# A two-layer hybrid backbone: the token mixers' TensorE work put in a fixed order, with split attention scores and stacked S5 halves

## The chip, the cores and the metric

The kernel runs on one core of one Trainium2 chip. The metric is device time in microseconds of one execution, from the core's first to its last instruction and what lies around it. Engines are named as in the profile: PE (TensorE matmul), PEld (its weight loads), DVE (VectorE), ACT (ScalarE), POOL (GpSimd), SP (the queue that issues most transfers).

## The reference

Two layers act on 256 latent tokens and 256 context tokens, 1024 channels wide, batch 1, all in float32. Each layer is a half-step SwiGLU feed-forward block (hidden width 2816), a block of parallel token mixers, and another half-step feed-forward block. Every block's input is normalised and modulated by vectors made from a conditioning vector; its output is scaled by a modulation gate, added to the stream and normalised.

The mixer block projects its modulated input once (`w_in`) into five parts and runs three branches on them:

- **S5**: 16 groups of 16 channels, a bidirectional complex diagonal state space with 64 states each; the scan over the context tokens hands its state to the latent tokens. A tanh-GELU and a gated linear unit (`w_glu`) follow.
- **FNet**: a 2-D DFT over positions and the 64 channels of each of 4 groups, real part.
- **Neighbourhood attention**: 8 heads of 64 channels, axial rotary position code, a window of 8 rows by 16 columns with a learned bias, plus all 256 context keys in the same softmax. In the first layer the context tokens attend among themselves too; the last layer makes no context output, so its queries, FNet and gates cover 256 tokens and not 512.

Each branch is projected to 1024 channels, multiplied by its own sigmoid gate (three gate vectors from `w_in`), the three are summed and projected by `w_out`.

## The kernel before

**Precision.** A large product is made of three matmuls on float32r parts: the weights (`chunk`, L79 and L80) and the activations are split into a high and a low part, and `mm3` (L87 to L89) issues high by high, high by low, low by high. Small products (S5, the DFT, attention scores and values) are plain float32 matmuls; a row of the profile with `x2` or `x8` counts two matmul records for each of those.

**The mixer in stages.** `mixer` opens a *front*: a main stream and side streams. The main stream is `main()`: the projections for S5 and half of the values (`tiled`, PSUM tile `pgm`), FNet (`pgf`), then for each of four head pairs the keys (`pgk`) and queries (`pgq`), the other half of the values, and the gate columns of the first output tiles (`pgg`, `gate_cols`). In the first layer (T = 512) the front prepares gate tiles 0 and 1, in the second (T = 256) tiles 0, 1 and 2. `interleave` advances the main stream by one yield a round (12 matmuls of 512 columns, or 24 of 256), and then each side stream whose count has run down; a yielded number is the rounds until its next turn.

The side streams are `ssm_stream` (S5 in two halves of 128 channels: eight transposes `psu` per half, then for each of four units `ssm_s2`, tile `psv`, and `ssm_s3`, tile `psy`, then GELU in `ssm_half` and eight transposes `psyt`; at the end `glu`, tile `psz`), `fnet` (`psf`, `pso`), one `attention` stream for each head pair, and `more`, which runs the steps of `extra` every third round.

`attention` takes a pair's keys and queries from PSUM, turns them by the rotary code (`rope`), and goes through jobs (head, query tile): `softmax_x` issues one float32 scores matmul (64 rows by 512 columns, tile `pss`) and the softmax on DVE and ACT; `softmax_c` does so for the context queries (two matmuls of 256 columns, `psc`); `transpose_p` turns the probabilities (`ppt`). At each turn it issues the scores of the next job and the transposes of the current one:

```
first(0)
for j in range(len(jobs)):
    yield 1
    if j + 1 < len(jobs):
        first(j + 1)
    second(j)
yield 1
nc.scalar.copy(yN[:, pair, :T], pv()[:, :T])
```

`pv` multiplies by the values (tile `po`): two heads in two column halves of the array, alternating.

`merge` follows: all branch outputs are split into `bh` (L1286, L1287), and for each of eight output tiles `d` it issues the gate columns of `d + 1`, then the three branch products (`pdb`), which DVE multiplies with the gates and adds. Then `w_out` (`pd` from `yT`) with the block's end.

**Modulation.** `mod(l, n)` makes 512 modulation values on DVE: four steps, each a 512 KB load on the SP queue into one of four `raw` buffers that weights share, and four products of 512 elements with a sum (L190). The first layer's mixer is given five such vectors (`M(0, 11, 16)`, 20 steps) as `extra`; the second's none.

**Order.** Nothing in the program fixes the order on any engine, apart from a few marked places: a list scheduler orders each engine's instructions ahead of time by program order as priority, by its own estimate of when operands are ready, and by free buffers. The order in the program is only a preference there. PSUM in the front: three buffers `psg`, three `psa` (scores, transposes, `po`), two `pss` (S5, and scratch of `mod`).

Of the kernel before, what the change touches and what calls it, by code (L numbers as in the profile page):

```python
# [8 lines left out]
F32 = mybir.dt.float32  # L9
F32R = mybir.dt.float32r  # L10
# [8 lines left out]
KT = 8  # L19
# [4 lines left out]
S_C, S_T, S_R, SN = 512, 1088, 1600, 1604  # L24


class Kernel:
    def __init__(self, tc, ctx, I, out):
# [8 lines left out]
        self.held = {}  # L37
        self.ctxs = ctx.enter_context(ExitStack())
# [137 lines left out]
    def mod(self, l, n):  # L176
# [7 lines left out]
        for b in range(4):  # L184
            raw = self.wraw.tile([128, 1024], F32, name="raw", tag="raw")
            nc.sync.dma_start(raw, I["w_modT"][l, n, b])
            junk = self.side([128, 512], "pj")
# [633 lines left out]
    def ssm_s2(self, l, pool, u, U):  # L821
# [13 lines left out]
        H = T("H", [128, 4, 64], 2)  # L835
# [3 lines left out]
        for c in range(4):  # L839
            g = 2 * (u % 4) + c % 2  # L840
            rhs = U[:, g].rearrange("p (h n) -> p h n", h=2)[:, ::-1, :] if c < 2 else U[:, g, ::-1]
# [16 lines left out]
        return st, mt, H, U  # L858

    def ssm_s3(self, u, q, yh, NR):  # L860

        nc = self.nc
        st, mt, H, U = q
        ca = st[:, S_C:S_C + 576].rearrange("p (c j k) -> p c j k", c=4, j=9)
        py = self.pss.tile([128, 128], F32, name="psy", tag="s")
        for i in range(3):
            for g in range(2):
                lhs, rhs = ((U[:, 2 * (u % 4) + g], mt[:, g]), (H[:, g], ca[:, g, 1:9]),
                            (H[:, 2 + g], ca[:, 2 + g, 0:8]))[i]
                nc.tensor.matmul(py[64 * g:64 * g + NR], lhs[:, :NR], rhs, start=i == 0, stop=i == 2,  # L870
                                 tile_position=(0, 64 * g))
        for g in range(2):
            ch = 32 * (u % 4) + 16 * g
            nc.scalar.copy(yh[:NR, :, ch:ch + 16], py[64 * g:64 * g + NR].rearrange("n (t c) -> n t c", t=8))

    def ssm_stream(self, l, pool, zt, yS, T):

# [3 lines left out]
        yh = {}  # L881
# [3 lines left out]
        yield 6 if l == 0 else 4  # L885

        def load(hf):
            zr = pool.tile([64, 8, 128], F32, name="zr", tag="ga", bufs=1)
            nc.sync.dma_start(zr, zv[:, :, 128 * hf:128 * hf + 128])
            Zs = pool.tile([64, 8, 8, 16], F32, name="Zs", tag="Zs", bufs=1)  # L890
            nc.scalar.copy(Zs, zr.rearrange("n s (g c) -> n g s c", g=8)[:, :, ::-1])
            yh[hf] = pool.tile([64, 8, 128], F32, name="yh", tag="yh", bufs=1)
            yield 1
            pu = self.pss.tile([128, 8, 64], F32, name="psu", tag="s")
            for g in range(8):
                nc.tensor.transpose(pu[:, g], Zs[:, g].rearrange("n s c -> n (s c)"), self.ident[:64, :64])
            U = pool.tile([128, 8, 64], F32, name="U", tag="U", bufs=1)
            nc.scalar.copy(U, pu)
            yield 1
            return U  # L900

        q = {}
        for hf in range(2):
            U = yield from load(hf)
            for u in range(4 * hf, 4 * hf + 4):
                q[u] = self.ssm_s2(l, pool, u, U)
                yield 1
                if u % 4:
                    self.ssm_s3(u - 1, q.pop(u - 1), yh[hf], NR)
                    yield 1  # L910
            self.ssm_s3(u, q.pop(u), yh[hf], NR)
            yield from self.ssm_half(l, pool, yh[hf], yS[:, hf, :T], NR)
        yield 1
        self.glu(l, pool, yS, T)

# [591 lines left out]
```

## Time and profile before

| | us |
|---|---|
| median of three runs (2030.26 to 2035.7) | 2033.48 |
| the profiled execution | 2028.64 |
| its span, first to last instruction | 2026.9 |
| first layer's front, 412.7 to 626.2 | 213.5 |
| first layer's merge, 626.2 to 768.3 | 142.1 |
| second layer's front, 1570.4 to 1733.0 | 162.6 |
| second layer's merge, 1733.0 to 1805.0 | 72.0 |

Starts are counted from the span's first instruction. A matmul's record is longer than the time until the next one starts, since matmuls are pipelined; so the cost of a matmul in a stream is read as the distance between two starts, and a busy PE can still be going slowly.

### The profile page before, as it was taken

The numbers are of one execution on the slowest core, as the hardware profiler recorded it, in microseconds if no ns is written. First come the engines' busy times: TensorE is split into PE (matmuls) and PEld (weight loads), VectorE is DVE, ScalarE is ACT, GpSimd is POOL, SyncE is SP. The second block draws the span as 40 slices with busy tenths as digits, with TensorE's granted clock in tenths as the row PEclk, the third lists the DMA queues.
The fourth block names the chain that finished last, engine by engine and source line by source line (L and its number), as shares of the span: only waits on it lengthen the run. The fifth ranks groups of instructions, "written<-read, shape, count | busy, mean of one in ns | idle before, by whom it ended". The sixth has DMA issues, their size and how long they took to land.

```text
span 2026.9 us, 27725 instructions
## 1 busy us (share of the span) xinstructions
PE 1970.7 (97%) x10072; PEld 1613.4 (80%) x10072; DVE 1526.9 (75%) x3405; ACT 777.1 (38%) x1253; POOL 111.6 (6%) x185
## 2 busy tenths in 40 slices
PE   7999999999999999999999999999999999999997
PEld 4888887787767887888888878888887977987886
DVE  4996899868997337876899688669768787775555
ACT  4322232355654224422233243222224566544442
POOL 0000100011000000100000010000001110000000
PEclk9999999999999999999999999999999999999999
DMA  8445556455344323345465625446543643664563
GB/s 317 151 148 156 174 200 206 151 175 171 118 145 140 104 88 123 124 152 181 154 209 184 221 94 187 156 155 206 171 159 117 200 150 124 206 218 149 185 179 122
DMA packets 103113, 333.03 MB, mean 164 GB/s; under 512 B 12352, under 2 KB 25504, under 8 KB 102976
## 3 DMA queue, kind: packets, MB, share of 16 engines
q1 hardware_dynamic: 96384, 310.96, 47.1%
q10 hardware_dynamic: 3584, 14.24, 1.9%
q0 software_dynamic: 3008, 6.07, 1.0%
q8 instruction: 79, 1.29, 0.3%
q14 instruction: 58, 0.48, 0.1%
HBM read 313.70 MB, written 17.51 MB: 163 GB/s over the span
## 4 chain that ended last, share of the span: by engine, by line
PE 59%; DVE 7%; issue 3%; DMA 2%; ACT 2%; POOL 1%; SPq 0%; POOLq 0%; ACTq 0%; DVEq 0%
PE pg L87 4%; PE pu L87 4%; PE pg L88 4%; PE pu L88 4%; PE pu L89 4%; PE pg L89 4%; PE pd L89 4%; PE pd L88 4%; PE pd L87 4%; PE pgg L87 3%; PE pgg L89 3%; PE pgg L88 3%; PE pgu L87 2%; PE pgu L88 2%; PE pgu L89 2%
## 5 line engine op out<-in xcount | busy, mean ns | idle before, releaser
L79 ACT CAST whi<-raw 128x1024 fp32r<-128x1024 f32 (+1 forms) x380 | 390.7, 1032 | 615.6 <-PE pd L89 154.9
L80 DVE TENSOR_TENSOR wlo<-raw,whi 128x1024 fp32r<-128x1024 f32 (+1 forms) x380 | 454.1, 1198 | 213.5 <-ACT whi L79 210.1
L190 DVE SCALAR_TENSOR_TENSOR pj<-raw,cb 128x512 f32<-128x512 f32 x512 | 350.5, 704 | 48.7 <-DMA raw<-in_w_modT 45.1
L87 PE MATMUL pd<-whi,gT 128*128 128x512 f32 x616 | 240.8, 391 | 0.4 <-DVE ev L273 0.4
L88 PE MATMUL pd<-wlo,gT 128*128 128x512 f32 x616 | 240.6, 391 | 0.5 <-DVE wlo L80 0.5
L89 PE MATMUL pd<-whi,gT 128*128 128x512 f32 x616 | 239.4, 389 | 0.0
L87 PE MATMUL pg<-uhi,whi 128*128 128x512 f32 (+1 forms) x560 | 215.1, 384 | 4.6 <-ACT uhi L247 4.4
L89 PE MATMUL pg<-uhi,wlo 128*128 128x512 f32 (+1 forms) x560 | 211.8, 378 | 2.7 <-DVE wlo L80 2.7
L87 PE MATMUL pu<-uhi,whi 128*128 128x512 f32 (+1 forms) x560 | 212.3, 379 | 1.3 <-DVE q L294 1.3
L88 PE MATMUL pg<-ulo,whi 128*128 128x512 f32 (+1 forms) x560 | 212.3, 379 | 0.0
L88 PE MATMUL pu<-ulo,whi 128*128 128x512 f32 (+1 forms) x560 | 211.8, 378 | 0.0
L89 PE MATMUL pu<-uhi,wlo 128*128 128x512 f32 (+1 forms) x560 | 211.7, 378 | 0.0
L87 PEld LDWEIGHTS pd<-whi,gT 128*128 128x128 f32 x616 | 115.6, 188 | 26.3 <-DVE ev L273 0.8
L88 PEld LDWEIGHTS pd<-wlo,gT 128*128 128x128 f32 x616 | 115.7, 188 | 24.6 <-DVE wlo L80 1.2
L89 PEld LDWEIGHTS pd<-whi,gT 128*128 128x128 f32 x616 | 115.7, 188 | 23.9
L87 PE MATMUL pgg<-uhi,whi 128*128 128x512 f32 (+1 forms) x384 | 131.8, 343 | 0.0
L89 PE MATMUL pgg<-uhi,wlo 128*128 128x512 f32 (+1 forms) x384 | 130.2, 340 | 0.5 <-DVE wlo L80 0.4
L88 PE MATMUL pgg<-ulo,whi 128*128 128x512 f32 (+1 forms) x384 | 129.7, 338 | 0.0
L87 PEld LDWEIGHTS pg<-uhi,whi 128*128 128x128 f32 x560 | 106.2, 190 | 28.9 <-ACT uhi L247 4.9
L89 PEld LDWEIGHTS pg<-uhi,wlo 128*128 128x128 f32 x560 | 105.9, 189 | 22.4 <-DVE wlo L80 3.1
L87 PEld LDWEIGHTS pu<-uhi,whi 128*128 128x128 f32 x560 | 106.2, 190 | 21.3 <-DVE q L294 1.5
L88 PEld LDWEIGHTS pg<-ulo,whi 128*128 128x128 f32 x560 | 105.9, 189 | 20.5 <-issue 1.2
(600 smaller groups left out, 3469.5 us busy)
## 6 DMA issues: line engine op xcount, KB each, us to landing
raw<-in_w_gu SPq DMA_DIRECT2D x132, 512.0 KB
raw<-in_w_modT SPq DMA_DIRECT2D x128, 512.0 KB
raw<-in_w_dn SPq DMA_DIRECT2D x80, 512.0 KB
raw<-in_w_in SPq DMA_DIRECT2D x80, 512.0 KB
raw<-in_w_gul SPq DMA_DIRECT2D x44, 512.0 KB
sd<-sst ACTq DMA_DIRECT2D x16, 802.0 KB
sst<-sd SPq DMA_DIRECT2D x16, 802.0 KB
wm<-in_w_mod SPq DMA_DIRECT2D x16, 512.0 KB
```

Of the source, the lines that this page charges most:

```text
L79: nc.scalar.copy(hi[:, :m], raw[:, :m])
L80: nc.vector.tensor_sub(lo[:, :m], raw[:, :m], hi[:, :m].bitcast(F32))
L87: mm(ps, a[0], b[0], start=start, stop=False)
L88: mm(ps, a[0], b[1], start=False, stop=False)
L89: self.last = mm(ps, a[1], b[0], start=False, stop=stop)
L190: V.scalar_tensor_tensor(junk, raw[:, 512 * k:512 * k + 512], 1.0, self.cb[:, s, 512 * k:512 * k + 512], op0=OP.mult, op1=OP.mult, accum_o ...
```

## The change

It touches the two mixers only:

1. From the second round of `main` on, the front runs under `manual_schedule` for PE, and so does `merge`: PE takes its instructions in program order. The other engines are scheduled as before.
2. Attention becomes one stream over all pairs. A `turn` stream rotates each `k` and `q` and splits it into float32r parts (`turned`, `split`), ready two rounds later. `scores` issues three matmuls per head, the two heads of a pair alternating (rows 0 to 63 and 64 to 127 of the array), at the first head's job; the transposes of a job come two rounds after its softmax was issued, and `po` follows a pair's last transposes by a round.
3. The two S5 halves share 128 partitions: one copy, one GELU, eight full transposes in and eight out. A unit takes two rounds. Its table tile is split: `sta` (two buffers) and `stc` (one buffer); `mt` and `H` have one buffer where they had two.
4. The 20 modulation steps of the first layer move from the front into `merge`, at the ends of `d` = 1 to 6, as five generators of five steps. Their loads go out on the POOL queue, in halves of 256 KB into three buffers of `merge`'s own, and the scratch output is in SBUF.
5. In `merge` the gate columns of `d + 1` are spread between the branch products; the second half of the values is projected before the fourth pair instead of the third.

```
-S_C, S_T, S_R, SN = 512, 1088, 1600, 1604
+S_T, S_R, S_C, SN = 512, 1024, 1028, 1604
...
-            for s in range(2):
+            if not self.mpool:
+                raw = self.wraw.tile([128, 1024], F32, name="raw", tag="raw")
+                nc.sync.dma_start(raw, I["w_modT"][l, n, b])
+                raw = raw[:, :512], raw[:, 512:]
+                junk = self.side([128, 512], "pj")
+            else:
+                raw = [self.mpool.tile([128, 512], F32, name="mraw", tag="mraw", bufs=3) for k in range(2)]
                 for k in range(2):
-                    V.scalar_tensor_tensor(junk, raw[:, 512 * k:512 * k + 512], 1.0, self.cb[:, s, 512 * k:512 * k + 512],
+                    nc.gpsimd.dma_start(raw[k], I["w_modT"][l, n, b][:, 512 * k:512 * k + 512])
+                junk = self.mpool.tile([128, 512], F32, name="mjunk", tag="mjunk", bufs=1)
+            for k in range(2):
+                for s in range(2):
+                    V.scalar_tensor_tensor(junk, raw[k], 1.0, self.cb[:, s, 512 * k:512 * k + 512],
                                            op0=OP.mult, op1=OP.mult, accum_out=res[:, k, s, b:b + 1])
-            if b < 3:
+            if b < 3 or self.mpool:
...
-        st = T("sst", [128, SN], 2)
-        nc.sync.dma_start(st, self.sd[l, u])
-        mt = T("mt", [128, 2, 128], 2)
+        st, so = T("sta", [128, S_C], 2), T("stc", [128, SN - S_C])
+        nc.sync.dma_start(st, self.sd[l, u][:, :S_C])
+        nc.sync.dma_start(so, self.sd[l, u][:, S_C:])
+        mt = T("mt", [128, 2, 128])
...
-        H = T("H", [128, 4, 64], 2)
+        H = T("H", [128, 4, 64])
...
+        U = pool.tile([128, 8, 2, 64], F32, name="U", tag="U", bufs=1)
+        for i in range(2):
+            pu = self.pss.tile([128, 4, 2, 64], F32, name="psu", tag="s")
+            for g in range(4):
+                nc.tensor.transpose(pu[:, g].rearrange("p h n -> p (h n)"),
+                                    Zs[:, 4 * i + g].rearrange("n s c -> n (s c)"), self.ident)
+            nc.scalar.copy(U[:, 4 * i:4 * i + 4], pu)
+        yh = pool.tile([128, 8, 128], F32, name="yh", tag="yh", bufs=1)
+        q = None
+        for u in range(8):
+            if q:
+                self.ssm_s3(u - 1, q, yh, NR)
+            q = self.ssm_s2(l, pool, u, U)
+            yield 2
+        self.ssm_s3(u, q, yh, NR)
...
+        yield 3
+        for i in range(2):
+            pt = self.pss.tile([128, 4, 128], F32, name="psyt", tag="s")
+            for t in range(4):
+                nc.tensor.transpose(pt[:, t, :N2], yh[:N2, 4 * i + t], self.ident[:N2, :N2])
...
+    def scores(self, outs, kk, qq, ks, qs):
+        mm = self.nc.tensor.matmul
+        for i, (a, b) in enumerate(((0, 0), (0, 1), (1, 0))):
+            for hh in range(2):
+                r = slice(64 * hh, 64 * hh + 64)
+                mm(outs[hh], qq[a][r, qs], kk[b][r, ks], start=i == 0, stop=i == 2)
+    def scores_x(self, qt, kk, qq):
+        ps = [self.psa.tile([128, 512], F32, name="pss", tag="a") for hh in range(2)]
+        self.scores(ps, kk, qq, slice(0, 512), slice(128 * qt, 128 * qt + 128))
+        return ps
+    def scores_c(self, kk, qq):
+        ps = [self.psa.tile([128, 2, 256], F32, name="psc", tag="a") for hh in range(2)]
+        for qt in range(2):
+            self.scores([x[:, qt] for x in ps], kk, qq, slice(256, 512), slice(256 + 128 * qt, 384 + 128 * qt))
+        return ps
...
+    def turned(self, pool, src, nm, scale, n):
+        hi, lo = (pool.tile([128, 512], F32R, name=nm + x, tag=nm + x, bufs=2) for x in "hl")
+        if n == 512:
+            nc.scalar.activation(hi[:, 256:], src[:, 256:], AF.Copy, scale=scale)
+            nc.vector.scalar_tensor_tensor(lo[:, 256:], src[:, 256:], scale, hi[:, 256:].bitcast(F32),
+                                           op0=OP.mult, op1=OP.subtract)
+        self.split(hi[:, :256], lo[:, :256], self.rope(pool, src[:, :256], scale))
+        return hi, lo
...
+        n = 6 if T == 512 else 4
+        jobs = [(pair, i, hh) for pair in range(4) for i in range(n // 2) for hh in range(2)]
...
+            pair, i, hh = jobs[j]
+            if hh == 0:
+                kk, qq = kq[pair, "k"], kq[pair, "q"]
+                S[0], S[1] = self.scores_x(i, kk, qq) if i < 2 else self.scores_c(kk, qq)
+            P[j] = self.softmax_x(l, pool, 2 * pair + hh, i, S[hh]) if i < 2 else self.softmax_c(pool, S[hh])
...
+        last, done = len(jobs) - 1, 0
+        for j in range(last + 3):
+            if done and done % n == 0:
+                pv(done // n - 1)
+            if 2 <= j <= last + 1:
+                second(done)
+                done += 1
+            if j <= last:
+                while (jobs[j][0], "q") not in kq:
+                    yield 1
+                first(j)
+            elif j == last + 1:
+                yield 1
+                second(done)
+                done += 1
             yield 1
...
-                def more():
-                    for step in extra:
-                        yield 3
-                        step()
+                def turn(kq, pair, ps, x, n):
+                    r = self.turned(pool, ps, x, 0.125 if x == "q" else 1.0, n)
+                    yield 2
+                    kq[pair, x] = r
+                    yield 0
...
-                    for pair in range(0, 2):
+                    kq = {}
+                    sides.append([1, self.attention(l, pool, kq, v, yN, T)])
+                    for pair in range(4):
+                        if pair == 3:
+                            yield from moving([W(3)], [store_v(1)], (0, 1))
                         w = W(4 + pair)
-                        pk = self.psg.tile([128, 512], F32, name="pgk", tag="g")
-                        yield from stationary(w, 0, 512, pk)
-                        pq = self.psg.tile([128, 512], F32, name="pgq", tag="g")
-                        yield from stationary(w, 1, T, pq)
-                        sides.append([1, self.attention(l, pool, pk, pq, v, yN, pair, T)])
-                    yield from moving([W(3)], [store_v(1)], (0, 1))
-                    for pair in range(2, 4):
-                        w = W(4 + pair)
-                        pk = self.psg.tile([128, 512], F32, name="pgk", tag="g")
-                        yield from stationary(w, 0, 512, pk)
-                        pq = self.psg.tile([128, 512], F32, name="pgq", tag="g")
-                        yield from stationary(w, 1, T, pq)
-                        sides.append([1, self.attention(l, pool, pk, pq, v, yN, pair, T)])
+                        for c, n, x in ((0, 512, "k"), (1, T, "q")):
+                            ps = self.psg.tile([128, 512], F32, name="pg" + x, tag="g")
+                            yield from stationary(w, c, n, ps)
+                            sides.append([1, turn(kq, pair, ps, x, n)])
...
-                self.interleave(main(), sides)
+                m = main()
+                next(m)
+                with self.tc.manual_schedule(engines={mybir.EngineType.PE}):
+                    self.interleave(m, sides)
...
+                    with self.tc.manual_schedule(engines={mybir.EngineType.PE}):
+                        self.merge(l, self.pool(e2, f"m3{l}"), (yS, yF, yN), yT, T, stationary, mo, th, extra)
...
+        self.spare, self.mpool = (self.psd, "d"), pool
...
-            if len(ths) <= d < KT - 1:
-                for _ in self.gate_cols(l, d + 1, T, stationary):
-                    pass
+            gates = self.gate_cols(l, d + 1, T, stationary) if len(ths) <= d < KT - 1 else iter(())
             y = pool.tile([128, 512], F32, name="ym", tag="ym", bufs=1)
             t = pool.tile([128, 512], F32, name="yt", tag="yt", bufs=1)
             for b, (j0, j1) in enumerate(spans):
+                for _ in range((0, 0, 2)[b] if d % 2 else (1, 0, 0)[b]):
+                    for _ in range(T // 256):
+                        next(gates, None)
...
+            if 1 <= d < KT - 1:
+                for step in extra[len(extra) * (d - 1) // 6:len(extra) * d // 6]:
+                    step()
+            for _ in gates:
+                pass
...
-        self.mixer(0, al, (0, 4), M(0, 11, 16))
+        self.mixer(0, al, (0, 4), self.steps([self.mod(0, n) for n in range(11, 16)], 5))
```

## Rows read from the trace of the kernel before

**Rows 1.** The page, part 1: busy us (share of the span) xinstructions.
```profile
PE 1970.7 (97%) x10072; PEld 1613.4 (80%) x10072; DVE 1526.9 (75%) x3405; ACT 777.1 (38%) x1253; POOL 111.6 (6%) x185
```

**Rows 2.** Stretches: us, busy PE, PEld, DVE, ACT, POOL, PEclk, DMA.
```profile
412.70:626.20 213.50, 208.44 (x1194) 156.99 (x1195) 182.31 (x494) 113.72 (x264) 17.53 (x39) 0.98 0.49 158
626.20:768.30 142.10, 142.10 (x624) 116.54 (x623) 63.87 (x76) 43.14 (x57) 0.00 (x0) 1.00 0.31 104
1570.40:1733.00 162.60, 159.71 (x1144) 131.90 (x1145) 124.78 (x289) 100.01 (x223) 18.27 (x38) 1.00 0.51 162
```

**Rows 3.** Waits of PE, first front (412.7:626.2): us, times, longest.
```profile
PE psv L842 <- DMA sst<-sd: 2.1, 2, 1.8
PE psu L896 <- ACT Zs L891: 2.1, 1, 2.1
```

**Rows 4.** Waits of PE, second front (1570:1733).
```profile
PE psv L842 <- DMA sst<-sd: 1.4, 2, 1.3
...
PE ppt L1042 <- DVE aq L1010: 0.4, 1, 0.4
```

**Rows 5.** Timeline of PE: start us, us, engine, line, operation, out<-in, count.
```profile
499.85 1.13 PE L1024 MATMUL psc__4665<-kr,qr 64*128 64x256 f32 x4
500.91 0.39 PE L88 MATMUL pgm<-wlo,uhi 128*128 128x256 f32 x1
501.13 0.28 PE L89 MATMUL pgm<-whi,ulo 128*128 128x256 f32 x1
...
505.60 1.12 PE L1002 MATMUL pss__4758<-kr,qr 64*128 64x512 f32 x2
506.65 0.38 PE L88 MATMUL pgm<-wlo,uhi 128*128 128x256 f32 x1
```

**Rows 6.** Timeline of PE around the GLU matmuls.
```profile
560.73 3.60 PE L943 MATMUL psz<-yS,wglu 128*128 128x512 f32 x8
564.26 1.12 PE L1002 MATMUL pss__5339<-kr,qr 64*128 64x512 f32 x2
```

**Rows 7.** Stretch of matmuls 256 columns wide, columns as in Rows 2.
```profile
420.00:440.00 20.00, 20.00 (x163) 19.66 (x162) 13.96 (x30) 11.71 (x20) 1.49 (x9) 1.00 0.52 173
```

**Rows 8.** Timeline of PE around one group of S5 transposes.
```profile
508.23 0.71 PE L896 MATMUL psu<-ident,Zs 64*128 64x64 f32 x8
508.87 0.39 PE L87 MATMUL pgm<-whi,uhi 128*128 128x256 f32 x1
```

**Rows 9.** Stretch right after a wait, columns as in Rows 2.
```profile
480.80:484.20 3.40, 3.40 (x10) 2.62 (x10) 3.22 (x9) 0.00 (x0) 0.00 (x0) 0.50 0.00 0
```

**Rows 10.** DVE in the first front: line, operation, count, busy, mean ns.
```profile
L190 DVE SCALAR_TENSOR_TENSOR pj<-raw,cb 128x512 f32<-128x512 f32 x80 | 55.5, 711 | 0.2
...
L995 DVE TENSOR_TENSOR kr<-kr,kx 128x256 f32<-128x256 f32 x4 | 1.7, 418 | 0.1
```

**Rows 11.** Timeline of PE at the end of the first front.
```profile
617.82 1.95 PE L1082 MATMUL po<-PT,v 128*64 128x256 f32 x16
619.60 1.03 PE L1082 MATMUL po<-PC,v 128*64 128x256 f32 x8
...
625.95 0.39 PE L89 MATMUL pgg<-uhi,wlo 128*128 128x512 f32 x1
626.18 0.39 PE L87 MATMUL pdb<-bh,whi 128*128 128x512 f32 x1
```

**Rows 12.** Timeline of ACT at the same place.
```profile
620.68 0.59 ACT L1093 COPY yN<-po 128x512 f32<-128x512 f32 x1 [0.78 <-PE po L1082]
...
622.46 1.15 ACT L1286 ACTIVATE bh<-yS 128x512 fp32r<-128x512 f32 x2
```

**Rows 13.** Timeline of PE at the end of the second front.
```profile
1728.18 1.95 PE L1082 MATMUL po<-PT,v 128*64 128x256 f32 x16
...
1733.04 0.28 PE L87 MATMUL pdb<-bh,whi 128*128 128x256 f32 x1
```

**Rows 14.** DMA issues: KB each, median us to landing.
```profile
sprm<-in_ssm_bc POOLq DMA_DIRECT2D x16, 128.0 KB, 2.7
```

More of the change, by code (lines that the diff above doesn't have):

```diff
@@ L37, in __init__ @@
         self.held = {}
+        self.mpool = None
         self.ctxs = ctx.enter_context(ExitStack())
@@ L884, in ssm_stream @@
         nc.gpsimd.memset(self.msk[:, 0:1], 0.0)
[L885 to L900, printed above, removed]
@@ L902, in ssm_stream @@
-        q = {}
-        for hf in range(2):
[L904 to L912, printed above, removed]
-        yield 1
-        self.glu(l, pool, yS, T)
@@ L925, in ssm_half, with glu @@
         nc.vector.scalar_tensor_tensor(x, a, 1.0, x, op0=OP.add, op1=OP.mult)
-        yield 1
-        pt = self.pss.tile([128, 8, 64], F32, name="psyt", tag="s")
-        for t in range(8):
-            nc.tensor.transpose(pt[:, t, :NR], yh[:NR, t], self.ident[:NR, :NR])
-        nc.scalar.activation(yg.rearrange("p (n t) -> p t n", t=8), pt[:, :, :NR], AF.Copy, scale=0.5)
-    def glu(self, l, pool, yS, T):
+        yield 3
[3 more added lines that the diff above has]
+                nc.tensor.transpose(pt[:, t, :N2], yh[:N2, 4 * i + t], self.ident[:N2, :N2])
+            for hf in range(2):
+                nc.scalar.activation(yS[:, hf, :T].rearrange("p (n t) -> p t n", t=8)[:, 4 * i:4 * i + 4],
+                                     pt[:, :, NR * hf:NR * hf + NR], AF.Copy, scale=0.5)
+        yield 1
+        self.glu(l, pool, yS, T, w)
+    def glu(self, l, pool, yS, T, w):
         nc, I = self.nc, self.I
-        w = pool.tile([128, 2, 256], F32, name="wglu", tag="p", bufs=3)
-        nc.sync.dma_start(w, I["w_glu"][l])
         b = pool.tile([128, 2], F32, name="bglu")
@@ L954, in fnet @@
         nc, I = self.nc, self.I
[L955 removed]
+        cs = pool.tile([128, 128], F32, name="dft64", tag="rr", bufs=1)
         nc.sync.dma_start(cs, I["dft64"])
@@ L995, in rope, with split, softmax_x @@
         nc.vector.tensor_add(dst, dst, x)
-    def softmax_x(self, l, pool, h, qt, kr, qr):
+        return dst
+    def split(self, hi, lo, src):
+        self.nc.scalar.copy(hi, src)
+        self.nc.vector.tensor_sub(lo, src, hi.bitcast(F32))
+    def scores(self, outs, kk, qq, ks, qs):
[13 more added lines that the diff above has]
+        return ps
+    def softmax_x(self, l, pool, h, qt, ps):
         nc, I = self.nc, self.I
         V, sm = nc.vector, self.sm
-        b = 64 * (h % 2)
-        ps = self.psa.tile([128, 512], F32, name="pss_", tag="a")
-        nc.tensor.matmul(ps, qr[b:b + 64, 128 * qt:128 * qt + 128], kr[b:b + 64], start=True, stop=True)
         bias = pool.tile([128, 256], F32, name="bias", tag="bias", bufs=3)
@@ L1016, in softmax_x, with softmax_c @@
         return p
-    def softmax_c(self, pool, h, kr, qr):
+    def softmax_c(self, pool, ps):
         nc, V = self.nc, self.nc.vector
-        b = 64 * (h % 2)
-        ps = self.psa.tile([128, 2, 256], F32, name="psc_", tag="a")
-        for qt in range(2):
-            o = 256 + 128 * qt
-            nc.tensor.matmul(ps[:, qt], qr[b:b + 64, o:o + 128], kr[b:b + 64, 256:], start=True, stop=True)
         p = pool.tile([128, 512], F32, name="pc", tag="p", bufs=3)
@@ L1217, in main @@
                             pass
-                    sides.append([2, more()])
                     yield
@@ L1275, in mixer, with merge @@
                         self.boundary(pool, nrm, t, nxt)
-    def merge(self, l, pool, ys, yT, T, stationary, mo, ths):
+    def merge(self, l, pool, ys, yT, T, stationary, mo, ths, extra):
         nc, I = self.nc, self.I
```

86 lines of the change are left out of this document (35 added, 51 removed).

## Prediction, written before the changed kernel was run

> **What bounds the kernel now.** I read the page's part 1 first: PE is busy for 97% of the span, DVE for 75% [rows 1]. A busy PE may be slow, so next came the stretches of the two mixers [rows 2]. In the first layer's front PE idles 5.1 of 213.5 us, in its merge not at all, in the second front 2.9 of 162.6. The list of PE's waits names what idle time there is: the S5 tables from DRAM (2.1 and 1.4 us), the S5 input copy (2.1), and hardly ever the softmax, 0.4 at most [rows 3, 4]. So both mixers are as long as what PE issues. The reader should see that a change to the order can win back only those few microseconds of waits; the rest must come from cheaper instructions or from fewer breaks in the main stream. The second point to see is DVE: 182.3 busy of 213.5 us in the first front (85%), 63.9 of 142.1 in the first merge [rows 2]. It runs close to PE in one stage and has room in the next.
>
> **Scores.** Distances between starts in the timeline of PE give the prices [rows 5]: a latent scores job costs 505.60 to 506.65, 1.05 us, a context job 499.85 to 500.91, 1.06. There are 4 pairs x 2 heads x 2 tiles x 2 layers = 32 and 8, together 33.6 + 8.5 = 42.1 us. The GLU's eight records, four float32 matmuls of 512 columns, take 560.73 to 564.26, 0.88 each [rows 6]; so 0.17 of a scores job is the switch into it. In the new form 16 visits issue six split matmuls of 512 columns and 4 visits twelve of 256. A split matmul of 512 costs 0.23 (625.95 to 626.18) [rows 11], one of 256 0.12 (163 in 20 us) [rows 7].
> Whether the two heads, in different row halves of the array, run at the same time is not in this trace. One bound: they don't. A latent visit is then 6 x 0.23 + 0.17 = 1.55 against 2.10, a context visit 12 x 0.12 + 0.17 = 1.61 against 2.12: 16 x 0.55 + 4 x 0.51 = 10.8 us saved. Other bound: they overlap fully, 0.86 and 0.89: 16 x 1.24 + 4 x 1.23 = 24.8. The nearest row is `po`, whose two heads alternate between column halves: 16 records of 256 columns take 617.82 to 619.60, 0.11 each [rows 11], while the GLU's cost 0.44 for 512, so 0.22 for 256 [rows 6]. Two halves did overlap there. I take overlap for the latent visits, but weight loads are a second limit: at 256 columns PEld is busy 19.66 of 20 us with 162 loads, 0.12 each [rows 7]. Six loads take 0.72, twelve 1.44: 0.89 and 1.61 a visit. Saved: 16 x 1.21 + 4 x 0.51 = **21.4**.
> The Trainium skill ("TensorE: Matmul & The Clock Gate", Part 3: Packing small matmuls) says that matmuls whose operands lie in different row groups run concurrently, and that a weight load overlaps matmuls in flight when its row group differs. By it context visits would be halved too and the sum would be near the upper bound, 24.8; no run here shows it.
>
> **S5 halves.** Each layer has two `psu` and two `psyt` groups of eight transposes, 0.64 a group (508.23 to 508.87) [rows 8]; it will have one of each, twice as wide. Saved: between 0 and 4 x 0.64 = 2.6; I take **2.0**, as a wider transpose may cost a little more. `psv` and `psy` stay. Half the GELU and copy work goes from DVE and ACT, off the path.
>
> **Breaks.** After a side visit the first main matmul is slow: 500.91 to 501.13 is 0.22 instead of 0.12 [rows 5, 7], so 0.10; with the switch into the visit (0.17) a break costs up to 0.27. From the streams' yields: before, the first front has 32 attention, 21 S5 and 4 FNet visits, the second 24, 21 and 2, 104 in all, each a turn of its own. After, all streams of a round follow one another. Counting rounds (40 of `main` in the first layer, 31 in the second), 34 and 24 rounds hold side work. 46 breaks fewer at 0.15: **6.9** (4.6 to 12.4).
>
> **Table waits.** `sta` has two buffers and a unit lasts two rounds, and its readers are done after the scan; so it can be fetched a unit ahead, where `sst` had to wait for `psy`. The 2.1 and 1.4 us go, and with the longest (1.8) the stretch behind it, 3.4 us at granted clock 0.50, the 1.2 GHz level [rows 9], which loses 1.7. I take **5.2** (0 to 5.2). `stc` and `mt`, with one buffer, are fetched during the same two rounds; queued behind them on SP are weights and bias tiles, two chunks ahead of PE. The S5 input wait stays.
>
> **Split work.** 28 turned blocks need a DVE subtraction of 256 columns, 0.42 [rows 10], 12 us in all, and as many ACT copies. PE hides them: DVE in the first front loses 55.5 us of products [rows 10]; in the second it goes from 125 of 163 to some 127 of 147 us (87%). Cost nothing; without that cover, at most the 5 us of the second front, and I put it under the waits below.
>
> **The ends of the fronts.** Today gate matmuls stand between the last `po` and the first `pdb`: from about 620.6 to 626.18, 5.6 us, and from 1730.1 to 1733.04, 2.9 [rows 11, 13]. In the new order gates are finished before the last pair's products, and `pdb` follows directly. What it waits for is short: copy of `po` (0.59), the split on ACT (0.57) and on DVE, about 2 us [rows 12]; in the second front also the copy of the last probabilities before `po`. Between 0 (the other six slices are ready early) and 8.5; I take **4.5 lost**, because `bh` was first written right after the `po` copy in the trace [rows 12].
>
> **Products in the merge.** DVE there goes from 63.9 to 63.9 + 55.5 = 119 of 142 us (84%), what the front ran at with few waits [rows 2, 4]. The loads move past SP, so weights no longer queue behind them; on POOL the nearest load took 2.7 us to land [rows 14]. If each of 20 steps held DVE for that, 119 + 54 = 173, 31 us over. Bounds 0 and 31; I take **2 lost**, and **3** for waits that the fixed order makes elsewhere (between 0 and the rival below). The later value projection costs nothing: `po` of pair 2 needs it two rounds after.
>
> **Sum.** 21.4 + 2.0 + 6.9 + 5.2 - 4.5 - 2 - 3 = 26.0 us. From the profiled execution, 2028.6, that is 2002.6; the median of the runs stands 4.8 above it, so I expect **2007**.
>
> **Rivals.**
> - *Row halves do not overlap*: the scores save 10.8, the time is 2018. For it: no row of before shows row halves together. Against: column halves do.
> - *The merge becomes DVE's*: its products are late and weights or PSUM buffers with them. At 40% of the bound, +12: 2019. For it: six output tiles carry all products, (63.9/8 + 55.5/6) = 17.2 of 17.8 us each. Against: no order fixes DVE's queue.
> - *More is won*: context visits overlap (+2.9), breaks cost 0.27 (+5.5), ends and order cost nothing (+7.5): 1991. The Trainium skill's rule above speaks for the first of these.
> - *The fixed order stalls PE, slower than before*: PE may no longer take gate or projection matmuls while a softmax, a rotation or a PSUM buffer is late. There are 71 rounds; from 29 us, 0.41 a round, the gain is gone. At 0.6 a round, 42.6 us, the time is 2047. For it: three `psa` buffers serve scores, transposes and `po`, so the second head's scores can wait for the copy of `po`. Against: two rounds (about 8 us) lie between a softmax and its transposes, and PE's longest softmax wait was 0.4 [rows 4].
>
> **Numbers.** A measurement of this kernel tells about 0.3%, 6 us, from no change: 2027.4 to 2039.6. Chances: forecast 0.56 (own range 1999 to 2014), no overlap 0.13, merge 0.10, more won 0.08, stalls 0.13, of which 0.05 for a size that ends within 0.3% and 0.08 for more. Faster: 0.56 + 0.13 + 0.10 + 0.08 = 0.87, less 0.02 for two of the bad cases at once: 0.85. Within: 0.05 + 0.02 = 0.07. Slower: 0.08. The range runs from 1993, short of the fullest gain, to 2027, which holds no overlap together with most of a late merge; it leaves out the stalls and most of "more won".
>
> **What would show it.** Right: a pair of latent scores visits near 0.9 us from its first start to the next instruction's, no wait on the S5 tables, first front near 197 us and second near 151, merges still 142 to 144 and 72, DVE above 80% in the first merge. Wrong: a visit at 1.5; PE's list of waits led by `ppt`, `pss` or `pdb`; stretches of granted clock 0.50 at the ends of the fronts; the first merge over 150 us.

## The result, and the profile after

The changed kernel takes 2007.5 us (median of 4 runs, 2005.3 to 2008.7) against 2033.2 of the kernel before beside it: a ratio of 0.9873, 95% interval 0.9856 to 0.9890. The forecast was 2007, its range 1993 to 2027. The profiled execution took 2008.24, its span is 2006.5.

The stretches that answer to [rows 2], with the second merge as well (us, busy PE, PEld, DVE, ACT, POOL, PEclk, DMA):

```profile
413.60:606.70 193.10, 188.25 (x1208) 152.78 (x1208) 137.51 (x335) 111.44 (x267) 20.16 (x42) 1.00 0.42 132
606.70:750.80 144.10, 142.46 (x626) 117.10 (x627) 116.47 (x249) 45.53 (x61) 20.26 (x38) 1.00 0.50 160
1552.90:1708.80 155.90, 149.01 (x1145) 130.67 (x1145) 123.97 (x293) 98.76 (x225) 18.55 (x38) 1.00 0.55 172
1708.80:1775.40 66.60, 66.52 (x552) 66.33 (x553) 47.53 (x77) 36.56 (x57) 0.00 (x0) 1.00 0.58 185
```

The first front is 20.4 us shorter, the second 6.8. DVE has 45 us less in the first front and 53 more in the merge, which is 1.7 longer. To the first `pd` matmul the second merge takes 66.7 us; the same distance before was 68.0. The four stages together are 26.8 us shorter, the medians of the runs 25.6. The two spans differ by only 20.4: from that `pd` to the end, before's profile has 225.8 us and this one 231.0. Of these 5.2 us, 3.3 come with the change. The span ends after a DRAIN on POOL, and that takes longer now (L1503 is the kernel before, L1547 the changed one; shortest, median and longest duration in ns):

```profile
L1503 POOLq DRAIN  x3: 40/102/7041, 2019.0 to 2026.6; - x3
L1547 POOLq DRAIN  x3: 40/93/10307, 1995.4 to 2006.2; - x3
```

The long one, 7.04 us or 10.31, starts in both 2.9 us before DVE's last instruction ends, and the span ends 4.9 or 8.2 us after that instruction. In the profiles of all kernels below it takes 7.04 us where the products run in the first front and 10.31 where they run in the merge. In the first case the program issues 66 transfers on POOL's queue, in the second 106, the 40 product loads more. 0.08 us for each of the 40 is an estimate from these two figures; no run shows whether the DRAIN goes by their number. The other 1.9 us are less clear: to the end of the last matmul this part takes 214.3 to 216.7 us in the four profiles with the products in the front and 216.0 to 218.3 in the ten others.

PE's waits in the first front, then in its merge, then in the second front (us, times, longest), to be held against [rows 3, 4]:

```profile
PE pgm L88 <- DVE nv L216: 1.4, 1, 1.4
PE ppt L1067 <- DVE p L1045: 1.1, 1, 1.1
PE psc L1017 <- ACT p L1042: 0.8, 1, 0.8
PE psc L1017 <- ACT PT L1068: 0.5, 1, 0.5
...
PE pgg L88 <- ACT th L1161: 1.4, 1, 1.4
PE pdb L88 <- ACT bh L1323: 1.2, 1, 1.2
...
PE psy L880 <- DVE H L866: 2.5, 3, 1.4
PE ppt L1067 <- DVE aq L1043: 1.7, 1, 1.7
```

No S5 table is in these lists any more, and the 2.1 us on the S5 input [rows 3] are gone too. New are short waits on a softmax, on `psa` buffers (`psc` behind an ACT read) and on the scan's `H`; the merge waits 1.4 us for a gate buffer that a tanh frees.

The timeline of PE at two latent visits and a context visit answers to [rows 5], the last two lines to [rows 11]:

```profile
576.69 0.50 PE L1017 MATMUL pss<-kh,qh 64*128 64x512 f32 x2
577.02 0.39 PE L1017 MATMUL pss<-kl,qh 64*128 64x512 f32 x2
577.26 0.39 PE L1017 MATMUL pss<-kh,ql 64*128 64x512 f32 x2
577.58 0.50 PE L88 MATMUL pgg<-uhi,whi 128*128 128x512 f32 x1
...
587.08 0.67 PE L1017 MATMUL pss<-kh,qh 64*128 64x512 f32 x2
587.41 0.57 PE L1017 MATMUL pss<-kl,qh 64*128 64x512 f32 x2
587.65 0.57 PE L1017 MATMUL pss<-kh,ql 64*128 64x512 f32 x2
588.14 0.50 PE L88 MATMUL pgg<-uhi,whi 128*128 128x512 f32 x1
...
594.73 0.39 PE L1017 MATMUL psc<-kh,qh 64*128 64x256 f32 x2
594.96 0.28 PE L1017 MATMUL psc<-kl,qh 64*128 64x256 f32 x2
595.08 0.27 PE L1017 MATMUL psc<-kh,ql 64*128 64x256 f32 x2
...
595.63 0.50 PE L88 MATMUL pgg<-uhi,whi 128*128 128x512 f32 x1
...
604.44 1.03 PE L1111 MATMUL po<-PC,v 128*64 128x256 f32 x8
606.72 0.50 PE L88 MATMUL pdb<-bh,whi 128*128 128x512 f32 x1 [1.24 <-ACT bh L1323]
```

The first latent visit lasts 0.89 us, and ten of the sixteen take 0.89 or 0.90. In the other six (1.06 to 1.67; the second one shown lasts 1.06) the second head starts 0.17 to 0.78 us behind the first; in all six the trace has it start behind an ACT read of a `psa` buffer, five times the copy of a `po` (`yN`). The eight of the first front average 7.78 / 8 = 0.97. The context visit shown, twelve matmuls, lasts 0.90; of the four, two are like that, and two take 1.82 and 2.10, again with a late second head. The first front ends with PE waiting 1.24 us for `bh`.

### The profile page after: what moved, and what is told of

It reads as the page before. It is cut to its first block, busy times and chain, and to the rows that moved or that the text cites. A ratio compares the mean times of both kernels' runs of the same rounds, so it can differ in the third digit from the quotient of the medians.

```text
span 2006.5 us, 27884 instructions
## 1 busy us (share of the span) xinstructions
PE 1941.8 (97%) x10088; PEld 1611.0 (80%) x10088; DVE 1533.7 (76%) x3427; ACT 776.9 (39%) x1267; POOL 134.7 (7%) x225
## 4 chain that ended last, share of the span: by engine, by line
PE 76%; DVE 13%; issue 4%; ACT 4%; DMA 2%; POOL 2%; POOLq 0%; SPq 0%; ACTq 0%; DVEq 0%
PE pg L88 6%; PE pd L90 6%; PE pd L89 6%; PE pd L88 6%; PE pu L88 6%; PE pg L89 6%; PE pg L90 6%; PE pu L89 6%; PE pu L90 6%; PE pgg L88 3%; PE pgg L90 3%; PE pgg L89 3%; DVE wlo L81 2%; PE pgu L88 2%; PE pgu L90 2%
## 5 line engine op out<-in xcount | busy, mean ns | idle before, releaser
L198 DVE SCALAR_TENSOR_TENSOR pj<-raw,cb 128x512 f32<-128x512 f32 x432 | 294.5, 702 | 52.6 <-DMA raw<-in_w_modT 49.3
L88 PEld LDWEIGHTS pu<-uhi,whi 128*128 128x128 f32 x560 | 106.8, 191 | 21.4 <-DVE q L302 1.5
```

The costliest lines, as they stand in the source:

```text
L88: mm(ps, a[0], b[0], start=start, stop=False)
L198: V.scalar_tensor_tensor(junk, raw[k], 1.0, self.cb[:, s, 512 * k:512 * k + 512], op0=OP.mult, op1=OP.mult, accum_out=res[:, k, s, b:b + 1])
```

## The experiments

Stage lengths (us) are distances between the starts of the first `pgm`, the first `pdb` and the first `pd` of each layer, from one profiled execution of each kernel. Ratios are to runs of the kernel before on the same chip, five rounds each; their intervals are 0.001 to 0.002 to either side.

| kernel | front 1 | merge 1 | front 2 | merge 2 | ratio |
|---|---|---|---|---|---|
| before | 213.5 | 142.4 | 162.7 | 68.0 | 1 |
| changed | 193.1 | 144.1 | 155.9 | 66.7 | 0.9873 |
| changed, again | 193.1 | 144.0 | 155.9 | 66.7 | 0.9885 |
| 1 scheduler's order | 194.5 | 142.3 | 156.0 | 68.7 | 0.9905 |
| 2 float32 scores, paired | 192.7 | 145.1 | 158.0 | 66.7 | 0.9913 |
| 3 heads not alternating | 193.2 | 143.9 | 155.7 | 66.7 | 0.9889 |
| 4 products in the front | 227.4 | 142.1 | 155.9 | 66.7 | 1.0024 |
| 5 as 4, scheduler's order | 210.1 | 142.1 | 155.6 | 67.2 | 0.9958 |
| 6 split scores, heads apart | 202.1 | 143.9 | 159.7 | 66.7 | 0.9955 |
| 7 before, order fixed | 241.8 | 151.9 | 192.3 | 72.3 | 1.0381 |
| 8 before, products in merge | 209.4 | 153.8 | 164.0 | 68.2 | 1.0050 |
| 9 as 8, order fixed | 223.2 | 162.3 | 196.8 | 72.3 | 1.0363 |
| 10 as 2, one table tile | 192.4 | 144.7 | 160.3 | 67.1 | 0.9902 |
| 11 as 3, merge 1 scheduler's | 193.5 | 143.8 | 155.7 | 66.7 | 0.9878 |

Kernels 1 to 4 ran on one chip, the others and the repeated changed kernel on another.

> The changed kernel without an edit, beside the next three on their chip. If the first four experiments' ratios (0.989 to 0.991, and 1.002 for the products in the front) show what their edits cost, this one gives the ratio it had at first, 0.987. If chips differ by as much as those edits, it gives 0.989 to 0.991.

It gave 0.9885 [0.9871, 0.9898]. So ratios within some 0.002 of it are not told apart from it.

**1. The order left to the scheduler.** `manual_schedule` is taken away in fronts and merges.

```
-                m = main()
-                next(m)
-                with self.tc.manual_schedule(engines={mybir.EngineType.PE}):
-                    self.interleave(m, sides)
+                self.interleave(main(), sides)
...
```

> The changed kernel with PE's order left to the scheduler again, in front and merge. Theory (the gain is in the array: overlapping row halves, fewer breaks; the order itself pays with bare ends and DVE waits about what it wins in breaks): breaks come back, +4 to +8 us, the ends of the fronts and the softmax and H waits go, -3 to -7: 2004 to 2013 us. Rival (the fixed order is what won the 26 us): 2020 or more.

2007.5 us, 0.9905 [0.9889, 0.9922]; no front differs by more than 1.4 us. The time is the theory's, and the rival fell. But the theory's breaks did not come back: PE changes from a main-stream matmul to one of a side stream 35 and 25 times in the two fronts, against 34 and 24 in the changed kernel and 56 and 41 before. So the new streams have fewer breaks in the scheduler's order too. With these streams, fixing the order is worth at most some 0.3%, and the runs don't show that it is worth anything.

**2 and 6. What makes scores cheap: the pairing or the split?** Number 2 issues float32 scores of both heads in the same visits and drops the split of `k` and `q`. Number 6 keeps the three split matmuls, but each head's stand in the round of its own softmax. The edit of number 2:

```
-        for i, (a, b) in enumerate(((0, 0), (0, 1), (1, 0))):
-            for hh in range(2):
-                r = slice(64 * hh, 64 * hh + 64)
-                mm(outs[hh], qq[a][r, qs], kk[b][r, ks], start=i == 0, stop=i == 2)
+        for hh in range(2):
+            r = slice(64 * hh, 64 * hh + 64)
+            mm(outs[hh], qq[r, qs], kk[r, ks], start=True, stop=True)
...
```

and in number 6, with `scores` for one head:

```
...
-            if hh == 0:
-                kk, qq = kq[pair, "k"], kq[pair, "q"]
-                S[0], S[1] = self.scores_x(i, kk, qq) if i < 2 else self.scores_c(kk, qq)
+            kk, qq = kq[pair, "k"], kq[pair, "q"]
+            S[hh] = self.scores_x(hh, i, kk, qq) if i < 2 else self.scores_c(hh, kk, qq)
```

> The changed kernel with float32 scores, one matmul a head and tile in the same visits, without the split of k and q. Theory (row halves overlap also in float32, but each matmul is two records of its own half, so only the middle of four overlaps): a latent visit 1.5 x 0.88 + 0.17 = 1.5 us against 0.97, a context visit near 1.4 against 0.9: 8 to 10 us slower, 2015 to 2018. Rival A (float32 does not overlap, all of it is the split's): visits 2.1, 20 us slower, 2028. Rival B (overlap alone matters, the split is worth nothing): 2007 to 2010.

> The changed kernel with the split scores of one head at a time, each in the round of its own softmax, so that no two heads' scores stand next to each other. Theory (row halves that run together are the gain of the scores, the split is none): a head costs 3 x 0.23 + 0.17 = 0.86 us, two 1.72 against 0.97 paired; 16 x 0.75 + 4 x 0.88 = 15.5 us more than the unchanged one, a ratio some 0.0076 higher. Rival (the three passes instead of float32's are the gain): 0 to 3 us more.

Number 2: 2010.8 us, 0.9913 [0.9898, 0.9929]. Number 6: 2020.5, 0.9955 [0.9943, 0.9968], 13.2 us above the repeated changed kernel on its chip. PE's timeline, a float32 pair of number 2:

```profile
575.19 1.13 PE L1016 MATMUL pss<-kh,qh 64*128 64x512 f32 x4
576.25 0.50 PE L88 MATMUL pgg<-uhi,whi 128*128 128x512 f32 x1
```

And two visits of number 6, heads apart:

```profile
487.06 0.50 PE L1016 MATMUL pss<-kh,qh 64*128 64x512 f32 x1
487.40 0.39 PE L1016 MATMUL pss<-kl,qh 64*128 64x512 f32 x1
487.63 0.39 PE L1016 MATMUL pss<-kh,ql 64*128 64x512 f32 x1
...
493.39 0.49 PE L1016 MATMUL pss<-kh,qh 64*128 64x512 f32 x1
493.73 0.39 PE L1016 MATMUL pss<-kl,qh 64*128 64x512 f32 x1
493.96 0.39 PE L1016 MATMUL pss<-kh,ql 64*128 64x512 f32 x1
```

Two float32 heads take 1.06 us side by side (1.12 on average in the first front), as long as one alone before [rows 5]. Distances from each scores matmul to the next instruction, summed over both layers with their waits, are 42.1 us for float32 apart (before), 27.0 for float32 paired, 35.7 for split apart, and 22.0 for split paired (changed). Pairing is worth 13.7 to 15.1 us, the split 5.0 to 6.4. For number 2 my theory (float32 overlaps only in part, visits near 1.5) and rival A (not at all) fell. Rival B had the overlap right, but the split is not worth nothing, and 2010.8 lies just above its range. For number 6 the theory's 15.5 us came out as 13.2; its second half, a split without gain, is wrong by the same 5.0 to 6.4 us.

**3. The alternation.** Each head's three matmuls in a row, inside the same visit.

```
-        for i, (a, b) in enumerate(((0, 0), (0, 1), (1, 0))):
-            for hh in range(2):
+        for hh in range(2):
+            for i, (a, b) in enumerate(((0, 0), (0, 1), (1, 0))):
```

> The changed kernel with the split matmuls of one head before those of the other. Theory (only neighbours in different row halves overlap): a latent visit goes from three steps of 0.23 to five, 0.97 to 1.4 us, a context visit from 0.9 to 1.25: 7 to 9 us slower, 2014 to 2017. Rival (PE finds the overlap in whatever order): unchanged, 2007. Rival (the overlap is not what makes the visits short): unchanged, visits still 0.97.

2005.4 us, 0.9889 [0.9873, 0.9905]: no loss is measured, the theory fell. Which rival holds is told by the starts. The timeline of one such visit:

```profile
575.55 0.51 PE L1017 MATMUL pss<-kh,qh 64*128 64x512 f32 x2
575.88 0.40 PE L1017 MATMUL pss<-kl,qh 64*128 64x512 f32 x2
576.12 0.40 PE L1017 MATMUL pss<-kh,ql 64*128 64x512 f32 x2
576.45 0.50 PE L88 MATMUL pgg<-uhi,whi 128*128 128x512 f32 x1
```

The second head's first matmul is fourth in the program, but its record starts 0.01 us behind the first head's first (they are the two records of the first line), ahead of the program's second and third. So PE found the overlap in this order too.

**4 and 5. The products back in the first front**, through SP and the shared `raw` buffers, a step every second round; in number 5 without the fixed order.

```
+                def more():
+                    for step in extra:
+                        yield 2
+                        step()
...
+                    sides.append([2, more()])
...
-        self.mixer(0, al, (0, 4), self.steps([self.mod(0, n) for n in range(11, 16)], 5))
+        self.mixer(0, al, (0, 4), M(0, 11, 16))
```

> The changed kernel with the 20 product steps back in the first front, through SP and the shared buffers, a step every second round so that they end with it. DVE there would be busy 137.5 + 55.5 = 193 of 193 us. Theory (a fixed order on PE needs room on DVE): PE waits on H, softmax and splits, the first front 5 to 15 us longer and the merge 1 to 2 shorter: 2011 to 2021. Rival (the products fill gaps of DVE, as in the kernel before, where 85% cost PE nothing): 2005 to 2008.

> The changed kernel with the products in the first front, and without the fixed order: the scheduler places PE's instructions in fronts and merges. Theory (the products cost time only where PE may not take other matmuls while DVE is late): the first front is 195 to 203 us long, against 227.5 with the fixed order, the time 0.988 to 0.994 of before. Rival (DVE itself is the bound with the products in a shorter front, whatever the order): 215 us or more, a ratio of 0.999 or more.

Number 4: 2033.6 us, 1.0024 [1.0015, 1.0034]; number 5: 2021.6, 0.9958 [0.9945, 0.9972]. The first front's stretch in number 4:

```profile
412.20:639.70 227.50, 203.61 (x1210) 162.47 (x1210) 184.24 (x506) 112.05 (x267) 20.98 (x39) 0.94 0.49 157
```

PE's longest waits in it:

```profile
PE pgt L168 <- DVE mres L166: 4.7, 1, 4.7
PE psy L880 <- issue: 2.8, 1, 2.8
PE ppt L1067 <- DVE pc L1059: 2.4, 1, 2.4
PE ppt L1067 <- DVE p L1045: 2.4, 2, 1.7
```

The same stretch in number 5:

```profile
411.50:621.60 210.10, 196.38 (x1209) 158.18 (x1209) 184.50 (x506) 112.42 (x267) 19.97 (x39) 0.98 0.54 170
```

In number 4 PE idles 23.9 us instead of 4.9, and a mean clock of 0.94 over 227.5 us costs up to another 13.7: together 32.7 of the 34.3 lost. My theory for number 4 had the direction but 5 to 15 us; its rival fell. Under the scheduler, the same 184 us of DVE cost half of that, 17.0 (15.6 against number 1, its like without the products; the profiled execution of number 5 is its fastest, 2015.8). My theory for number 5 (195 to 203 us) was too low, the rival (215 or more) too high: the products are dear by themselves once the front has become short, and the fixed order doubles it.

That it is DVE's load is not shown. The longest wait of number 4 is PE's own transpose of the products' result (`pgt` behind `mres`, 4.7 us; 6.6 in number 7 below, 1.1 in number 5). With the products came back also their 512 KB loads on SP and their scratch output in the two `pss` buffers of S5. The runs don't separate these.

**7. Before, with the order fixed.** The edit of number 1 turned round, on the kernel before.

> The kernel before with only the order of PE's instructions fixed in fronts and merges: heads apart, float32 scores, products in the first front. Theory (a fixed order is dear while DVE carries the products, as it was when they were put back into the changed kernel: 34 us of first front): the first front goes from 213 to 235 us or more, the time to 2050 or more. Rival (the order itself is the gain, by fewer breaks): below 2025.

2108.1 us, 1.0381 [1.0366, 1.0395]. The first front is as foreseen. But the second front, which has no products, loses 30 us as well. Its stretch:

```profile
1611.30:1803.60 192.30, 171.13 (x1144) 141.55 (x1145) 126.45 (x289) 100.38 (x223) 18.89 (x38) 0.93 0.43 138
```

PE's longest waits there:

```profile
PE psv L842 <- DMA sst<-sd: 6.5, 4, 2.0
PE ppt L1042 <- DVE p L1015: 5.6, 4, 2.3
PE psyt L929 <- DVE yh L925: 4.4, 2, 2.7
```

Tables, softmax and GELU are late for PE in the program's old order; idle time is 21 us against 3, and the clock of 0.93 takes the rest. The merges are longer as well, by 9.5 and 4.3 us.

**8 and 9. Before, with the products moved alone**, then with the order fixed too: `mod`, `merge`'s steps, and the call of `mixer` from the change, all else as before.

> The kernel before with one part of the change alone: the products of the modulation go from the first front to the first merge. Theory (by itself the move is worth only what PE idles and loses to the clock in that front, 5.1 + 3.4 us at most): first front 205 to 212 us against 213.5, merge 142 to 145, ratio 0.996 to 1.000. Rival (DVE at 85% was a hidden limit of the first front): front 200 or less, ratio 0.993 or less.

> As the one above, and the order of PE's instructions fixed. Theory (a fixed order is dear with the old streams, whose transposes follow their softmax after one round, with or without the products): first front 230 us or more, second 190 as with the fixed order and products before (192.3), 2085 us or more. Rival (the products made the first front dear): first front 217 or less, about 2070 us.

Number 8: 2042.4 us, 1.0050 [1.0032, 1.0069], slower than before. The first front gains 4.1 us, as in the theory, but the first merge loses 11.4, which neither theory nor rival held; with the other stages that is 8.9 us, and the longer DRAIN adds 3.3. The merge's stretch:

```profile
623.50:777.30 153.80, 147.04 (x627) 118.58 (x626) 114.36 (x243) 42.38 (x56) 19.91 (x37) 0.98 0.48 153
```

PE's waits there:

```profile
PE pgg L88 <- ACT th L1132: 4.3, 3, 2.8
PE pdb L90 <- DVE wlo L81: 2.4, 2, 2.0
```

DVE has the same load as in the changed merge, and PE waits for gate buffers that a tanh frees late, and for weights that DVE splits late. Number 9: 2105.5, 1.0363 [1.0347, 1.0378]; the second front stays long, 196.8, as the theory said; the first, 223.2, lies between theory and rival; the merge grows to 162.3, with 14.6 us of the wait behind the tanh. So the old streams under a fixed order cost 30 to 33 us in the second front, and in the first 10 to 14 without the products and 28 with them.

**10. The S5 table in one tile.** On number 2, since its memory has room.

```
-        st, so = T("sta", [128, S_C], 2), T("stc", [128, SN - S_C])
...
+        st = T("sst", [128, SN], 2)
+        nc.sync.dma_start(st, self.sd[l, u])
+        so = st[:, S_C:]
```

> The changed kernel with float32 scores (as in the run of float32 scores above, so that the memory suffices) and the S5 table as one tile of two buffers again instead of two tiles. Theory (the split of the table removed the table waits): waits of PE on the table come back, 2 to 6 us, and the fronts go from 192.7 and 158.0 us to 195 to 198 and 160 to 162. Rival (the new streams removed them: the table's last reader of one unit now stands two rounds ahead of the first reader of the unit after next): no wait on the table, fronts as with float32 scores.

2011.4 us, 0.9902 [0.9887, 0.9916]; no wait on the table in either front. The rival holds in that the new streams removed those waits and the split of the tile did not. Moving the products away did not either: in number 8 PE still waits 2.0 and 2.4 us for the table. That it is the units' spacing is the likely reason, but it was not tried by itself. (The second front is 2.3 us longer than in number 2; its mean clock is 0.97 there against 0.99, worth up to 3.2 us of its 160.)

**11. First merge in the scheduler's order**, on number 3.

> The changed kernel with each head's split matmuls in a row, and the first merge in the scheduler's order. With the scheduler's order everywhere that merge was 142.3 us long against 144.05. Theory (the fixed order costs that merge 1.7 us): first merge 142 to 142.6, ratio 0.987 to 0.989. Rival (its length came with the other order of the front): 144 again.

2006.1 us, 0.9878 [0.9862, 0.9893]: merge 143.8, so the rival, and no better than the changed kernel by what can be measured.

## Why the prediction was right, and where it wasn't

The time was right, and so was the mechanism in the main: the scores of two heads run together, the breaks are fewer, the table waits are gone. That the time fits to half a microsecond is luck, as several terms missed and cancelled. By stages, the first front came out at 193.1 us where 197 was foreseen, the second at 155.9 where 151 was. And the sum was taken from a profiled execution of 2028.6 us; the changed kernel's took 2008.2, not 2002.6. The 4.8 us added for the median hold for before's profile; the changed kernel's lies 0.7 above its median. On the second chip the gain was 2030.2 - 2007.3 = 22.9 us, near the 26.8 of the stages less the 3.3 of the DRAIN.

Term by term in us saved, from distances between starts in the two traces. Breaks are the gain of the main stream's matmuls without idle time and without stretches at clock 0.50:

| term | foreseen | measured |
|---|---|---|
| scores | 21.4 | 20.1 (42.1 to 22.0) |
| S5 transposes | 2.0 | 1.8 (5.0 to 3.2) |
| breaks | 6.9 | 7.6 (3.8 in each front) |
| table waits and clock | 5.2 | 5.2 (3.5, and 1.7 for the half-clock stretch behind the longest) |
| S5 input wait and clock | 0 | 3.8 (2.1, and 1.7 for the half-clock stretch behind it) |
| ends of the fronts | -4.5 | -2.0 (1.2 and 0.8) |
| merges | -2 | -0.3 (1.7 longer, 1.4 shorter) |
| other waits | -3 | -8 (`psy` and `psv` 1.5 and 6.5 longer) |
| `po` and `ppt` without idle time | 0 | -1.4 |
| sum | 26.0 | 26.8, as in the four stages; smaller terms cancel |
| DRAIN at the end | 0 | -3.3 |

- **Scores.** The row halves overlap; numbers 2 and 6 show that this, and not the three passes, is most of the gain. The step "weight loads are a second limit", which priced a context visit at 1.61, failed: it took 0.90 where the second head was not late, since loads of the two halves overlap as well (they start 0.004 us apart in the context visit shown). By the Trainium skill ("TensorE: Matmul & The Clock Gate", Part 3: Packing small matmuls), a load overlaps matmuls of another row group; the 0.90 agrees, and the weight given to the 256-column stretch [rows 7], where all 128 rows are loaded, was misplaced. Undisturbed, the visits would so have taken 17.8 us instead of the 20.7 foreseen. What the prediction left out here is that a second head can be late: this cost 2.0 us in the latent and 2.1 in the context visits, 1.6 of it idle time of PE, and made 22.0.
- **Breaks.** Foreseen were 104 to 58, 46 fewer; counted are 97 to 58, 39 fewer, but at 0.2 us each instead of 0.15. Number 1 shows that the new streams have as few without the fixed order; with it, the old streams have 33 and 27 (number 7).
- **Ends of the fronts.** The copy and the split after the last `po` cost 1.2 and 0.8 us, half of what I took. I had the first product wait for the split on DVE too, about 2 us in all; it needs the high part alone, and the low part held PE 0.2 us more in the merge.
- **Other waits.** Mis-sized, 8 for 3, and nearly all of it in the second front, which so came out 5 us too long. PE idles 6.9 us there instead of 2.9: 2.5 for the scan's `H` and 1.7 for a softmax's `aq`, both from DVE, which is 80% busy. The rest of the 8, 2.7 us, is slower passage between the S5 matmuls and their new neighbours, so part of what the breaks gave stands here again. Why `H` is late (its single buffer, or DVE's queue) was not tried and stays open.
- **Table waits.** They went, but of the two reasons that I gave, two buffers of a smaller tile and two rounds for a unit, number 10 shows that the smaller tile has no part in it.
- **S5 input wait.** The prediction had it stay; it went, with the half-clock stretch at 450.1 that stood behind it. Together these are as much as the 4 us by which the first front came out shorter than foreseen. The wait is 0.4 us in number 8, where only the products moved, and 1.9 again in number 4, where they came back; but number 1 still has 1.3, so the cause is open.
- **Products.** I booked the move as a cost of 2 us and treated its relief as cover for the split work. The cost has a part that the sum left out, the 3.3 us of POOL's DRAIN. The relief is much larger: without the move the changed kernel loses 11 to 14 us (scheduler's order, number 5 against number 1 by ratios and by medians) or 28 us (fixed order, by 0.9885 against 1.0024), all in the first front. In the kernel before, the same move loses 11 us net. The rival "the merge becomes DVE's" had that mechanism and price (12 us foreseen, 11.4 measured in number 8); it did not come about, as the changed merge with the same load took 144. What cures it is not isolated: the changed merge spreads the gates between branch products, and number 1 (142.3, scheduler's order) shows that the fixed order is not the cure.
- **The stall rival.** "The fixed order stalls PE" was right of the old streams (ratio 1.0381, number 7) and wrong of the new ones while the products are in the merge; with them in the front it holds again (number 4 against 5). The step it named, a second head's scores late behind the copy of `po`, did happen, but cost 4.1 us and not 42.6. What stood against it in the prediction, two rounds between a softmax and its transposes, is in line with this; the new streams also differ in S5's spacing, and the two were not tried apart.

## What to carry to other kernels

Small matmuls with 64 rows are worth issuing next to a partner in the other row half before thinking about their precision: here the neighbour was worth 14 us and the cheaper passes 5. A fixed order is no gain in itself: with the new streams it did no harm as long as the products were out of the front, and with the old ones it turned 3 us of idle time into 21, with the clock lost on top. That the new streams bear it because operands are made two turns ahead is likely but not shown. Before costing a move of off-path work, ask what both stages would be without it: the same move was worth 11 to 28 us after the front had been shortened, and lost 11 before. When the parts of a sum are checked against stages, look at what lies behind the last stage too: here 3.3 us were lost there.

## What the runs showed of the hardware

- Matmuls in different row halves ran together even when the program issued all three of one head before the other's (number 3: starts 0.01 us apart, undisturbed visits 0.90 us against 0.89). In number 6, with a round between the heads, a visit pair cost 14.25 / 8 = 1.78 us instead of 0.97.
- Their weight loads overlap too: twelve matmuls of 256 columns with as many loads took 0.90 us, 0.075 each, where full-height loads took 0.12 each [rows 7].
- Idle time on PE comes with a second cost: in number 7's second front, 18 us more idle came with a mean granted clock of 0.93 over 192.3 us, worth up to another 13.5; the front was 29.6 us longer.
- The DRAIN on POOL at the end of the program took 7.04 us in all four profiles with 66 transfers on POOL's queue and 10.31 us in all ten with 106, and the span ended 3.3 us later.
